# Winograd block products: running sums in PSUM and all operand sums on VectorE

## The chip, the core and the metric

The kernel runs on one core of one Trainium2 chip. The time is the device time of one launch in microseconds (us). Three timed runs of the kernel before took 3626.16, 3637.07 and 3639.25 us, median 3637.07. The engines are named as in the profile: PE is TensorE's matmuls and PEld its weight loads, DVE is VectorE, ACT is ScalarE, POOL is GpSimd, SP is SyncE, which issues the loads.

## The reference, cut to what matters

Two transformer-like blocks, one after the other, on 1024 tokens of 1024 features in float32. The ten stretches that this document is about are three matrix products with 1024 output features: the down products of the three feed-forward nets, and the output product of the second block's mixer.

```python
# block 1
x = x + einsum("bte,ed->btd", mix, w_out)                # mix: gating, convolution, delta rule
h = rms_norm(x, ffn_norm_g)
ff = silu(h @ w_gate) * (h @ w_up)                       # 1024 -> 2816 features
x = x + ff @ w_down                                      # first down: 2816 -> 1024
x = rms_norm(x, final_norm_g)
# block 2
h = concatenate([meta_tokens, x])                        # 16 tokens more
h = h + 0.5 * swiglu(rmsnorm(h, ffn1_norm), w1, w3, w2)  # second down
...
h = h + merged @ w_out                                   # merged: attention and state space, gated
h = h + 0.5 * swiglu(rmsnorm(h, ffn2_norm), w1, w3, w2)  # third down
return rmsnorm(h, final_norm)[:, 16:]
```

## The kernel before

**Precision.** Every float32 operand is split in two parts, hi + lo: ScalarE copies it to a rounded hi, VectorE subtracts hi to get lo (`hilo`, L208 to L210; `wsplit`, L245 to L254, for weights). A product is then three matmuls, hi hi, hi lo and lo hi, for each of the 128-feature tiles of the inner sum (`product`, L460 to L468; the matmul is L467).

**Block products.** Tokens are kept as two halves of 512, features on the partitions. A product with 1024 outputs is a 2 x 2 block product (output halves r, inner halves c, token halves h), and `seven` computes it in Winograd's form: seven block products in place of eight, at the price of sums of weight blocks A[r, c] and of feature blocks B[c, h]. The down products are cut into three batches of 4, 3 and 4 feature tiles per inner half; the mixer's output product is one batch of 4. Each of a batch's seven products gives four output tiles of 128 features; with four inner tiles such a tile is 4 x 3 = 12 matmuls of 512 columns. The batches are called here a1, a2, a3 (first down), b1, b2, b3 (second down), c (mixer's output product) and d1, d2, d3 (third down). In the second down the 16 extra tokens make the first half 528 long, and every tile goes in two pieces of 264 columns.

**Operand sums.** `both` (L500 to L503, the sum itself is L503) makes a sum two inner tiles at a time, so 128x1024 (or 128x1056 for 528 tokens); they are called from `prepare` (L505 on), which makes the operands of a product while the one before it runs. `pools` (above `wblock`) says on which engine ten of the sixteen sums of a batch go: VectorE in a1 and a2, GpSimd in the other eight batches. Weight blocks are loaded into the pools `raw` and `s`, feature blocks into `s`; the next batch's are loaded into the slots of the blocks that have been used up.

**Residual sums.** Each output tile's product lies in a PSUM bank and is added to the residual tiles in SBUF, `hs[half][r]` (`add`, L579 to L583; L581 is the plain sum, L583 the one with a factor). Winograd's form needs partial sums that go to more than one place: a tile x in SBUF takes product 1 by a ScalarE copy (L608), then 6 and 7 are added into it, and x is added to residuals from there. Per output tile that is nine adds on VectorE and two on the engine in `pools`. The PSUM buffers `pd` (three) and `pq` (three) take turns; `ps` (two) is used by other steps, among them the state space's matrices, which are traced beside the first feed-forward net.

**Beside it.** In the last batch of each product, finished residual tiles go to the sums of squares of the next norm (`Stat`, its add on GpSimd is L98; the norm's factors come from matmuls at L404 to L409), and in d3 through the final norm's transposes (`Final`, L108). A scheduler fixes each engine's instruction order when the kernel is built; each engine then runs its list in order.

## Time and profile before

| | |
|---|---|
| timed runs, median (lowest to highest) | 3637.07 us (3626.16 to 3639.25) |
| profiled execution, span | 3629.7 us |
| PE busy | 93% |
| DVE busy | 73% |
| POOL busy | 30% |

No time besides the span is recorded for the profiled execution; the median lies 7.4 us above that span. Shares are averages over the whole program, and the ten batches take 916 us of it together. For each batch a table below gives the busy time of the engines in that stretch, with the number of instructions in brackets, the mean granted clock of TensorE (PEclk, 1.00 is 2.4 GHz) and the load on the DMA engines. A row of grouped instructions gives line, engine, operation, output and inputs with their shapes, the count, the busy time of all of them and the mean of one in ns, and after the second bar the idle time ahead of them with what ended it. Rows of the timeline give start and length in us, and in square brackets how long the engine had waited, and for what.

### The profile page before, as it was taken

How to read it: one execution, taken by the hardware profiler on the slowest of the kernel's cores; microseconds unless marked ns; L12 is line 12 of the kernel's file. 1: busy time of each engine (PE TensorE's matmuls, PEld its weight loads, DVE VectorE, ACT ScalarE, POOL GpSimd, SP SyncE). 2: the span in 40 equal slices, each digit the busy share in tenths (PEclk: the TensorE clock that was granted, in tenths of full speed). 3: DMA queues.
4: the chain of work that ended last, by engine and by line, in shares of the span. 5: the costliest groups of instructions: out<-in, count | busy, mean ns of one | idle time of the engine just before them, and what ended most of it. 6: DMA issues, size and time to landing. Idle time of an engine off the chain costs nothing.

```text
span 3629.7 us, 49236 instructions
## 1 busy us (share of the span) xinstructions
PE 3387.2 (93%) x18860; PEld 2877.8 (79%) x18860; DVE 2632.0 (73%) x4371; ACT 1398.0 (39%) x2408; POOL 1091.8 (30%) x1199
## 2 busy tenths in 40 slices
PE   7989889999997978999999899999999889999988
PEld 6777777788886858999989888778777678888766
DVE  6886675866776998767689845644665986666997
ACT  4355344433332424333333435543554343333333
POOL 2332323200048254000045627300820740000555
PEclk9989999999998988999999999999999999999999
DMA  3312313222244312333353143136225222224321
GB/s 102 101 52 67 97 62 126 80 85 87 82 163 133 125 59 73 104 112 99 118 183 113 47 104 104 62 125 166 73 67 165 98 75 98 76 91 156 124 87 47
DMA packets 325097, 361.78 MB, mean 100 GB/s; under 512 B 43193, under 2 KB 240990, under 8 KB 324862
## 3 DMA queue, kind: packets, MB, share of 16 engines
q1 hardware_dynamic: 324862, 358.64, 31.0%
q8 instruction: 148, 2.42, 0.3%
q14 instruction: 87, 0.71, 0.1%
HBM read 282.75 MB, written 75.84 MB: 99 GB/s over the span
## 4 chain that ended last, share of the span: by engine, by line
PE 64%; DVE 19%; POOL 5%; issue 4%; ACT 2%; DMA 1%; SPq 0%; ACTq 0%; DVEq 0%; POOLq 0%
PE pd L467 35%; PE pd L277 16%; PE pq L467 4%; DVE wl L210 3%; DVE z L210 3%; DVE s L503 2%; DVE s L583 1%; DVE s L581 1%; DVE s L1377 1%; PE pq L1953 1%; PE pq L1993 1%; ACT wh L209 1%; POOL u L98 1%; DVE s L210 1%; PE pq L1952 1%
## 5 line engine op out<-in xcount | busy, mean ns | idle before, releaser
L277 PE MATMUL pd<-s,wh 128*128 128x512 f32 (+2 forms) x2720 | 859.6, 394 | 11.0 <-POOL s L210 5.4
L467 PE MATMUL pd<-z,wh 128*128 128x512 f32 (+1 forms) x2640 | 681.3, 346 | 40.7 <-DVE z L210 25.1
L209 ACT CAST wh<-raw 128x1024 fp32r<-128x1024 f32 (+1 forms) x424 | 439.5, 1039 | 680.6 <-PE pd L277 261.2
L210 DVE TENSOR_TENSOR wl<-raw,wh 128x1024 fp32r<-128x1024 f32 (+1 forms) x394 | 514.0, 1304 | 238.2 <-ACT wh L209 218.2
L467 PE MATMUL pd<-s,wh 128*128 128x512 f32 (+1 forms) x2560 | 635.2, 338 | 14.6 <-ACT wh L209 14.4
L277 PEld LDWEIGHTS pd<-s,wh 128*128 128x128 f32 x2720 | 508.8, 193 | 112.6 <-POOL s L210 6.7
L467 PEld LDWEIGHTS pd<-z,wh 128*128 128x128 f32 x2640 | 464.5, 193 | 103.5 <-DVE z L210 30.6
L277 PE MATMUL pd<-s,wl 128*128 128x512 f32 (+2 forms) x1360 | 534.4, 393 | 6.6 <-DVE wl L210 6.6
L467 PEld LDWEIGHTS pd<-s,wh 128*128 128x128 f32 x2560 | 440.4, 189 | 66.2 <-ACT wh L209 15.7
L467 PE MATMUL pd<-z,wl 128*128 128x512 f32 (+1 forms) x1320 | 455.6, 345 | 7.3 <-DVE wl L210 7.3
L467 PE MATMUL pd<-s,wl 128*128 128x512 f32 (+1 forms) x1280 | 432.9, 338 | 0.8 <-DVE wl L210 0.8
L467 PE MATMUL pq<-z,wh 128*128 128x512 f32 (+2 forms) x1360 | 357.7, 352 | 29.8 <-DVE s L583 22.8
L277 PEld LDWEIGHTS pd<-s,wl 128*128 128x128 f32 x1360 | 262.5, 193 | 55.1 <-DVE wl L210 7.4
L467 PEld LDWEIGHTS pq<-z,wh 128*128 128x128 f32 x1360 | 243.0, 196 | 61.3 <-DVE s L583 23.4
L467 PEld LDWEIGHTS pd<-z,wl 128*128 128x128 f32 x1320 | 254.3, 193 | 37.4 <-DVE wl L210 10.3
L467 PEld LDWEIGHTS pd<-s,wl 128*128 128x128 f32 x1280 | 241.6, 189 | 26.8 <-DVE wl L210 1.5
L467 PE MATMUL pq<-z,wl 128*128 128x512 f32 (+2 forms) x680 | 236.3, 347 | 0.0
L210 DVE TENSOR_TENSOR z<-s,z 128x1024 fp32r<-128x1024 f32 (+3 forms) x140 | 211.2, 1525 | 3.6 <-ACT z L209 3.6
L503 POOL TENSOR_TENSOR raw<-raw,s 128x1024 f32<-128x1024 f32 (+1 forms) x16 | 47.1, 2964 | 524.6 <-DMA s<-in_ffn_w_dram 398.6
L467 PE MATMUL pd<-s 128*128 128x512 f32 (+1 forms) x912 | 171.0, 336 | 0.0
L209 ACT CAST z<-s 128x1024 fp32r<-128x1024 f32 (+3 forms) x140 | 133.4, 989 | 74.3 <-DVE s L503 57.7
L98 POOL TENSOR_TENSOR u<-u,t 128x512 f32<-128x512 f32 (+4 forms) x95 | 124.8, 1321 | 114.6 <-ACT t L96 113.4
(470 smaller groups left out, 5373.9 us busy)
## 6 DMA issues: line engine op xcount, KB each, us to landing
raw<-in_w_in_dram SPq DMA_DIRECT2D x56, 1024.0 KB
raw<-in_ffn_w_dram SPq DMA_DIRECT2D x56, 1024.0 KB
ffd<-t SPq DMA_DIRECT2D x90, 256.0 KB
s<-ffd SPq DMA_DIRECT2D x16, 1024.0 KB
raw<-in_w_gate_dram SPq DMA_DIRECT2D x12, 1024.0 KB
raw<-in_w_up_dram SPq DMA_DIRECT2D x12, 1024.0 KB
raw<-in_w_out_dram SPq DMA_DIRECT2D x10, 1024.0 KB
s<-hd SPq DMA_DIRECT2D x10, 1024.0 KB
```

Source lines behind the costliest of these rows:

```text
L98: nc.gpsimd.tensor_tensor(acc, acc, s, op=ALU.add)
L209: self.nc.scalar.copy(hi, src)
L210: (eng or self.nc.vector).tensor_tensor(lo, src, hi.bitcast(F32), op=ALU.subtract)
L277: nc.tensor.matmul(out, a[:, k, :], b, start=c == 0, stop=c == 3 * kt - 1)
L467: self.nc.tensor.matmul(p[:, :n], a[:, k, :], b[:, k, t0 : t0 + n], start=c == 0, stop=c == 3 * kt - 1)
L503: eng.tensor_tensor(out[:, k], x[:, k], y[:, k], op=op)
L581: (eng or nc.vector).tensor_tensor(d, p, d, op=ALU.add)
L583: nc.vector.scalar_tensor_tensor(d, p, factor, d, op0=ALU.mult, op1=ALU.add)
L1377: nc.vector.scalar_tensor_tensor(a, y, f, a, op0=ALU.mult, op1=ALU.add)
L1952: nc.tensor.matmul(p[:, lo:272], Q[:, r, :], khi[:, cols], start=True, stop=False)
L1953: nc.tensor.matmul(p[:, lo:272], Q[hb : hb + 64, r, :], klo[hb : hb + 64, cols], start=False, stop=True)
L1993: nc.tensor.matmul(po[rr * 64 : rr * 64 + 64, j * 128 : (j + 1) * 128], v[b + s][:, g * 64 : (g + 1) * 64], PT[j][:, s, rr, :], start=Fals ...
```

## The change

It has three parts. First, where tokens go in one piece (a, c and d; `chained`), the products come in the order 1, 2, 6, 7, 4, 5, 3 (it was 1, 2, 4, 6, 7, 5, 3), and the results add up in PSUM: products 1, 6, 7 and 4 of an output tile go into one bank (`sums`, from pd, pd, pq, pq for the four tiles), 2 into another and 5 and 3 into one (`pairs`, from pd, pq, ps, ps). After each product its bank, with all that it holds by then, is added to one residual tile; there is no tile x, no copy into it, and there are seven adds per output tile. The operand sums are arranged anew for this order, with a further tile t1 = A10 + A11. Second, all operand sums are on VectorE, in all batches. Third, all residual sums are on VectorE too, also in the second down, which otherwise keeps the old form. The loads of the next batch stand at other products, and those of the second half's residual earlier. Most of the diff's remaining lines remove comments.

```diff
+        chained = len(pieces) == 1
+        order = (1, 2, 6, 7, 4, 5, 3) if chained else (1, 2, 4, 6, 7, 5, 3)
-        pools = [nc.vector if self.nff == 1 and z + 1 < len(batches) else nc.gpsimd for z in range(len(batches))]
...
-        def both(out, x, y, op, eng=nc.vector):
+        def both(out, x, y, op):
...
-                eng.tensor_tensor(out[:, k], x[:, k], y[:, k], op=op)
+                nc.vector.tensor_tensor(out[:, k], x[:, k], y[:, k], op=op)
+        def early(z):
+            t1[z] = self.S()[:, : batches[z] * 512].rearrange("p (k f) -> p k f", f=512)
+            both(t1[z], a[z, 1, 0], a[z, 1, 1], ALU.add)
...
-            if z == 0 and i == 4:
+            if z == 0 and i == (6 if chained else 4):
                 start(0, 1)
-            if z == 0 and i == 6:
+            if z == 0 and i == (2 if chained else 6):
                 start(1, 0)
                 start(1, 1)
...
+                wk = {1: (0, 0), 2: (0, 1), 6: (0, 0), 7: (1, 0), 4: (1, 1), 5: None, 3: (0, 1)}[i]
...
+            wv = A(*wk) if wk else t1[z]
...
+            if chained:
+                if i == 1:
+                    both(B(0, 0), B(0, 1), B(0, 0), ALU.subtract)
+                    early(z)
+                if i == 2:
+                    t2[z] = tile(kt)
+                    both(t2[z], B(1, 1), B(0, 0), ALU.subtract)
+                    both(A(1, 0), A(0, 0), A(1, 0), ALU.subtract)
+                    both(A(0, 0), t1[z], A(0, 0), ALU.subtract)
+                if i == 6:
+                    both(B(0, 1), B(1, 1), B(0, 1), ALU.subtract)
+                    both(B(1, 0), B(1, 0), t2[z], ALU.subtract)
+                if i == 7:
+                    both(A(0, 1), A(0, 1), A(0, 0), ALU.subtract)
+                    a[z, 0, 0] = t2[z] = None
+                    if nxt:
+                        wblock(nxt, 0, 0)
+                        fblock(nxt, 0, 0)
+                if i == 4:
+                    a[z, 1, 0] = b[z, 0, 1] = None
+                    if nxt:
+                        fblock(nxt, 1, 0)
+                        wblock(nxt, 0, 1)
+                if i == 5:
+                    a[z, 1, 1] = b[z, 1, 0] = None
+                    if nxt:
+                        wblock(nxt, 1, 1)
+                        fblock(nxt, 0, 1)
+                if i == 3:
+                    t1[z] = a[z, 0, 1] = b[z, 0, 0] = b[z, 1, 1] = None
+                    if nxt:
+                        wblock(nxt, 1, 0)
+                        fblock(nxt, 1, 1)
...
+                if chained:
+                    if i == 1:
+                        sums[u] = self.pd() if u < 2 else self.pq()
+                    if i in (2, 5):
+                        pairs[u] = (self.pd, self.pq, self.ps, self.ps)[u]()
+                    p = (sums if i in (1, 6, 7, 4) else pairs)[u]
+                    p = self.product(p, w, cur["x"], ta, n, batches[z], i in (1, 2, 5), i in (2, 4, 3), ta)
+                else:
+                    p = self.product(self.pd() if c % 2 else self.pq(), w, cur["x"], ta, n, batches[z])
...
+                if chained:
+                    add({1: ha, 2: ha, 4: ha}.get(i, hb)({1: 0, 2: 0, 6: 0, 7: 1, 4: 1, 5: 1, 3: 0}[i]), p)
...
                     elif i == 6:
                         add(s, p)
-                        add(hb(0), s[:, v:], pools[z])
+                        add(hb(0), s[:, v:], True)
                     elif i == 7:
                         add(s, p)
-                        add(ha(1), s, nc.vector)
-                        add(hb(1), s[:, v:], pools[z])
+                        add(ha(1), s, True)
+                        add(hb(1), s[:, v:], True)
```

The next two fences are VectorE's order at the start of d1, while product 1 runs and 2 begins: before, then after. L503 and L510 are the operand sums, L583 and L634 the adds to the residual, L210 the subtraction of a split, L816 and L885 the last of the gating.

```order
L583 SCALAR_TENSOR_TENSOR s<-pd,s 128x512
L816 TENSOR_TENSOR t<-t,u 128x512
L503 TENSOR_TENSOR s<-s 128x1024
L210 TENSOR_TENSOR wl<-s,wh 128x1024
L583 SCALAR_TENSOR_TENSOR s<-pq,s 128x512
L503 TENSOR_TENSOR s<-s 128x1024 x3
L583 SCALAR_TENSOR_TENSOR s<-pd,s 128x512
```

```order
L510 TENSOR_TENSOR s<-s,raw 128x1024
L885 TENSOR_TENSOR t<-t,u 128x512
L510 TENSOR_TENSOR s<-s,raw 128x1024
L634 SCALAR_TENSOR_TENSOR s<-pd,s 128x512
L210 TENSOR_TENSOR z<-s,z 128x1024 x2
L634 SCALAR_TENSOR_TENSOR s<-pd,s 128x512
L210 TENSOR_TENSOR wl<-s,wh 128x1024
L510 TENSOR_TENSOR s<-s 128x1024 x2
L510 TENSOR_TENSOR s<-raw,s 128x1024 x2
L510 TENSOR_TENSOR raw<-s,raw 128x1024 x2
L634 SCALAR_TENSOR_TENSOR s<-pq,s 128x512 x2
```

Eight operand sums stand here in place of four, and two of the residual adds wait behind six of them.

GpSimd's order in the third down, before and after; L98 is the add of squares, L746 and L210 belong to the gating's operands.

```order
L210 TENSOR_TENSOR s<-t,s 128x512
L503 TENSOR_TENSOR raw<-raw,s 128x1024 x2
L503 TENSOR_TENSOR s<-s,raw 128x1024 x2
L503 TENSOR_TENSOR s<-s 128x1024 x2
L503 TENSOR_TENSOR raw<-raw 128x1024 x2
L503 TENSOR_TENSOR s<-s,raw 128x1024 x2
L581 TENSOR_TENSOR s<-s 128x512 x8
```

```order
L746 TENSOR_TENSOR t<-s 128x512
L210 TENSOR_TENSOR s<-t,s 128x512
L98 TENSOR_TENSOR u<-u,t 128x512 x6
L98 TENSOR_TENSOR u<-u,t 128x256 x12
L2349 UNCONDITIONAL_BRANCH
```

Of three batches' sums nothing is left on GpSimd; between the gating and the squares of the last norm it has no work.

VectorE's order at the start of b2, where the form stays: before, then after.

```order
L210 TENSOR_TENSOR wl<-raw,wh 128x768
L583 SCALAR_TENSOR_TENSOR s<-pd,s 128x264
L210 TENSOR_TENSOR z<-s,z 128x1056
L210 TENSOR_TENSOR z<-s,z 128x528
L583 SCALAR_TENSOR_TENSOR s<-pq,s 128x248
L503 TENSOR_TENSOR s<-s 128x1056
L583 SCALAR_TENSOR_TENSOR s<-pd,s 128x264
L503 TENSOR_TENSOR s<-s 128x528
L583 SCALAR_TENSOR_TENSOR s<-pq,s 128x248
L210 TENSOR_TENSOR wl<-raw,wh 128x768
```

```order
L210 TENSOR_TENSOR wl<-raw,wh 128x768
L634 SCALAR_TENSOR_TENSOR s<-pd,s 128x264
L210 TENSOR_TENSOR z<-s,z 128x1056
L210 TENSOR_TENSOR z<-s,z 128x528
L634 SCALAR_TENSOR_TENSOR s<-pq,s 128x248
L634 SCALAR_TENSOR_TENSOR s<-pd,s 128x264
L510 TENSOR_TENSOR s<-s 128x1056
L634 SCALAR_TENSOR_TENSOR s<-pq,s 128x248
L210 TENSOR_TENSOR wl<-raw,wh 128x768
L634 SCALAR_TENSOR_TENSOR s<-pd,s 128x264
L510 TENSOR_TENSOR s<-s 128x528
L510 TENSOR_TENSOR raw<-raw,s 128x1024
```

The operand sums stand among the adds as before, and the weight sums (`raw<-raw,s`), which were GpSimd's, follow them.

## Rows read from the trace of the kernel before

**Rows 1.** The page, part 1: busy us, share of the span, instructions.

```profile
PE 3387.2 (93%) x18860; PEld 2877.8 (79%) x18860; DVE 2632.0 (73%) x4371; ACT 1398.0 (39%) x2408; POOL 1091.8 (30%) x1199
```

**Rows 2.** Windows, a1 to d3: length, busy PE, PEld, DVE, ACT, POOL, PEclk, DMA, GB/s.

```profile
1069.30:1193.70 124.40, 101.86 (x487) 84.45 (x486) 92.40 (x103) 34.95 (x53) 96.75 (x143) 0.89 0.45 144
1193.70:1251.80 58.10, 57.82 (x255) 47.56 (x254) 58.10 (x81) 25.61 (x33) 0.00 (x0) 1.00 0.46 156
1251.80:1368.00 116.20, 89.69 (x360) 72.52 (x359) 107.45 (x105) 38.46 (x50) 69.52 (x31) 0.88 0.14 46
1844.80:1937.50 92.70, 84.28 (x675) 83.15 (x675) 90.67 (x112) 29.82 (x37) 55.19 (x28) 0.98 0.45 149
1937.50:2009.70 72.20, 65.84 (x507) 65.01 (x506) 68.23 (x108) 26.05 (x36) 35.08 (x25) 0.95 0.31 104
2009.70:2101.00 91.30, 77.20 (x592) 76.48 (x592) 77.41 (x102) 37.36 (x64) 67.59 (x52) 0.91 0.14 47
2812.40:2911.00 98.60, 83.97 (x345) 67.18 (x344) 88.90 (x86) 37.33 (x47) 68.48 (x31) 0.91 0.27 96
3357.20:3442.90 85.70, 78.86 (x337) 64.30 (x336) 85.60 (x73) 26.39 (x29) 49.93 (x19) 0.96 0.39 133
3442.90:3509.30 66.40, 59.03 (x254) 46.96 (x254) 64.91 (x68) 24.90 (x33) 36.29 (x17) 1.00 0.35 119
3509.30:3620.00 110.70, 96.60 (x471) 79.18 (x469) 96.86 (x129) 38.57 (x55) 65.03 (x36) 0.94 0.05 20
```

**Rows 3.** Windows, stretches of d1 and b1 in which TensorE is never idle.

```profile
3404.90:3442.90 38.00, 38.00 (x169) 31.50 (x168) 37.90 (x39) 12.16 (x13) 18.95 (x9) 1.00 0.39 130
1890.90:1936.00 45.10, 45.10 (x374) 45.10 (x373) 43.07 (x66) 15.38 (x16) 18.91 (x19) 1.00 0.36 113
```

**Rows 4.** Groups on VectorE in a2, shapes kept apart: count, busy us, mean ns.

```profile
L581 DVE TENSOR_TENSOR s<-pq,s 128x512 f32<-128x512 f32 x15 | 10.0, 676 | 0.0
L210 DVE TENSOR_TENSOR z<-s,z 128x1024 fp32r<-128x1024 f32 x8 | 9.6, 1211 | 0.0
L210 DVE TENSOR_TENSOR wl<-raw,wh 128x768 fp32r<-128x768 f32 x6 | 5.7, 946 | 0.0
L503 DVE TENSOR_TENSOR s<-s 128x1024 f32<-128x1024 f32 x3 | 3.7, 1219 | 0.0
```

**Rows 5.** Groups on VectorE in d1 and d2, shapes kept apart.

```profile
L210 DVE TENSOR_TENSOR z<-s,z 128x1024 fp32r<-128x1024 f32 x20 | 32.6, 1638 | 0.0
L583 DVE SCALAR_TENSOR_TENSOR s<-pd,s 128x512 f32<-128x512 f32 x31 | 20.7, 676 | 0.0
L503 DVE TENSOR_TENSOR s<-s 128x1024 f32<-128x1024 f32 x9 | 20.0, 2243 | 0.0
```

**Rows 6.** Timeline, a stretch of b3: start, length, what, wait before it.

```profile
2018.77 0.42 DVE L583 SCALAR_TENSOR_TENSOR s<-pq,s 128x264 f32<-128x264 f32 x1
2019.12 0.41 DVE L583 SCALAR_TENSOR_TENSOR s<-pd,s 128x264 f32<-128x264 f32 x1
...
2022.30 3.32 POOL L503 TENSOR_TENSOR s<-s 128x1056 f32<-128x1056 f32 x1 [1.19 <-DVE s L503]
2023.28 8.00 DVE L503 TENSOR_TENSOR s<-s 128x1056 f32<-128x1056 f32 x3
2026.82 3.35 POOL L503 TENSOR_TENSOR s<-s 128x1056 f32<-128x1056 f32 x1 [1.20 <-DVE s L503]
...
2031.68 0.81 PE L467 MATMUL pq<-z,wh 128*128 128x264 f32 x2 [8.75 <-DVE s L583]
```

**Rows 7.** Waits of TensorE in b1 to b3: all us, count, longest.

```profile
PE pq L467 <- DVE s L583: 22.8, 9, 8.8
```

**Rows 8.** The chain that ended last, in order of time, end of a3.

```profile
1330.52 1.36 POOL s L581
...
1337.89 3.57 PE pq L409 x16
```

**Rows 9.** Windows, line L503 alone, whole span: DVE busy, then POOL busy.

```profile
0.00:3629.70 3629.70, 122.85 (x80) 230.88 (x80) 0.96 0.31 100
```

More of the change, by code (lines that the diff above doesn't have):

```diff
@@ L460, in norm_steps, with product @@
             yield from self.norm_apply(h, g, rB, t0, rB.shape[1], A)
-    def product(self, p, w, x, t0, n, kt=4):
+    def product(self, p, w, x, t0, n, kt=4, first=True, last=True, o=0):
         c = 0
@@ L466, in product @@
             for a, b in ((w[0], x[0]), (w[0], x[1]), (w[1], x[0])):
-                self.nc.tensor.matmul(p[:, :n], a[:, k, :], b[:, k, t0 : t0 + n], start=c == 0, stop=c == 3 * kt - 1)
+                self.nc.tensor.matmul(p[:, o : o + n], a[:, k, :], b[:, k, t0 : t0 + n], start=first and c == 0,
+                                      stop=last and c == 3 * kt - 1, skip_group_check=not (first and last))
                 c += 1
-        return p[:, :n]
+        return p[:, o : o + n]
     def seven(self, batches, weight, feature, residual, hs, pieces, factor, parts=None):
@@ L544, in prepare @@
             wv = xv = None
+            if chained:
[31 more added lines that the diff above has]
+                        fblock(nxt, 1, 1)
+                yield
+                return
             if i == 2:
@@ L557, in prepare @@
             if i == 6:
-                both(A(0, 1), A(0, 1), A(1, 1), ALU.subtract, pool)
+                both(A(0, 1), A(0, 1), A(1, 1), ALU.subtract)
                 t2[z] = a[z, 1, 1] = None
@@ L577, in prepare, with add @@
             yield
-        def add(d, p, eng=None):
-            if eng or factor == 1.0:
-                (eng or nc.vector).tensor_tensor(d, p, d, op=ALU.add)
+        def add(d, p, plain=False):
+            if plain or factor == 1.0:
+                nc.vector.tensor_tensor(d, p, d, op=ALU.add)
             else:
                 nc.vector.scalar_tensor_tensor(d, p, factor, d, op0=ALU.mult, op1=ALU.add)
-        items = [(z, i) for z in range(len(batches)) for i in (1, 2, 4, 6, 7, 5, 3)]
+        items = [(z, i) for z in range(len(batches)) for i in order]
         res, c = {}, 0
         drain(prepare(0, 1, res))
-        x = res.pop("X")
+        x = res.pop("X", None)
+        sums, pairs = {}, {}
         for e, (z, i) in enumerate(items):
@@ L591, in seven @@
             pre = prepare(*items[e + 1], res) if e + 1 < len(items) else iter(())
-            if i == 1 and z:
+            if i == 1 and z and not chained:
                 x = tile(4)
@@ L605, in seven @@
                 hb = lambda r: hs[1][r][:, u, tb + v : tb + n]
-                s = x[:, u, ta : ta + n] if i in (1, 6, 7) else None
-                if i == 1:
-                    nc.scalar.mul(s, p, factor)
-                    add(ha(0), p)
-                elif i == 2:
-                    add(ha(0), p)
-                elif i == 4:
-                    add(ha(1), p)
-                elif i == 6:
-                    add(s, p)
-                    add(hb(0), s[:, v:], pools[z])
-                elif i == 7:
-                    add(s, p)
-                    add(ha(1), s, nc.vector)
-                    add(hb(1), s[:, v:], pools[z])
-                elif i == 5:
-                    add(hb(1), p[:, v:])
-                    add(hb(0), p[:, v:])
-                else:
-                    add(hb(0), p[:, v:])
-                s = None
+                if chained:
+                    add({1: ha, 2: ha, 4: ha}.get(i, hb)({1: 0, 2: 0, 6: 0, 7: 1, 4: 1, 5: 1, 3: 0}[i]), p)
+                    if i == 4:
+                        sums[u] = None
+                    if i in (2, 3):
+                        pairs[u] = None if i == 2 or ta + n == 512 else pairs[u]
+                else:
+                    s = x[:, u, ta : ta + n] if i in (1, 6, 7) else None
+                    if i == 1:
+                        nc.scalar.mul(s, p, factor)
+                        add(ha(0), p)
+                    elif i == 2:
+                        add(ha(0), p)
+                    elif i == 4:
+                        add(ha(1), p)
+                    elif i == 6:
+                        add(s, p)
+                        add(hb(0), s[:, v:], True)
+                    elif i == 7:
+                        add(s, p)
+                        add(ha(1), s, True)
+                        add(hb(1), s[:, v:], True)
+                    elif i == 5:
+                        add(hb(1), p[:, v:])
+                        add(hb(0), p[:, v:])
+                    else:
+                        add(hb(0), p[:, v:])
+                    s = None
+                p = None
                 if u == 1 and tb + n == 512:
@@ L631, in seven @@
                         next(pre, None)
-                yield i if last else 0, u, ra, rb
+                yield ({7: 4, 4: 7}.get(i, i) if chained else i) if last else 0, u, ra, rb
             cur = None
```

22 lines of the change are left out of this document (11 added, 11 removed).

## The prediction

> **What bounds the kernel now.** I read the shares first, then a table of the ten batches of block products in question, then the stretches in which TensorE runs undisturbed, then VectorE's operations one by one, once without and once beside GpSimd. The shares [rows 1] call TensorE the bound: 93% busy, VectorE 73%, GpSimd 30%. But the shares average over the program, and the change touches ten batches only: three of the first feed-forward block (a1 to a3), three of the second (b1 to b3), one of the mixer's output product (c), three of the third block (d1 to d3). In their table [rows 2] VectorE is the crowded one: busy for 85.60 of 85.70 us in d1, 90.67 of 92.70 in b1, 107.45 of 116.20 in a3.
>
> What would TensorE need? In undisturbed stretches 168 matmuls of 512 columns take 38.0 us and 372 of 264 columns 45.1 us [rows 3], so 0.226 and 0.121 each (the x counts there include the one cut by the edge). A batch with four feature tiles has 7 products of 4 tiles of 12 matmuls, 336: a floor of 76.0 us. With three tiles it is 252: 57.0. In the second block, in two pieces of 264, the floors are 81.5 and 61.1. Against these the batches lose [rows 2]: a1 48.4, a2 1.1, a3 40.2, b1 11.2, b2 11.1, b3 9.8, c 22.6, d1 9.7, d2 9.4, d3 34.7; all but a1 and a2: 148.7 us. (a1's loss is largely the state space's matrices traced beside it; a3's, c's and d3's hold norms and transposes too.)
>
> Why is VectorE crowded? Without GpSimd at work, in a2, a hi/lo subtraction of 128x1024 takes 1211 ns and an operand sum 1219 [rows 4]. In d1 and d2, beside GpSimd's sums, the same subtraction takes 1638 and the same sum 2243, while an add that reads one operand from PSUM keeps its 676 [rows 5]. So only operations with both inputs in SBUF stretch. One place shows it [rows 6]: three sums, worth 3 x 1.2 = 3.7 us alone, take 8.00 while GpSimd runs sums of 3.32 and 3.35 us, and TensorE has stood still for 8.75 us when it resumes at 2031.68, waiting for the add behind them. Over b1 to b3 TensorE waits 22.8 us for such adds [rows 7]. GpSimd's queue costs in a second way: in a3's chain the norm's matmuls at 1337.89 follow residual sums on GpSimd [rows 8].
>
> **What is removed.** Of GpSimd: 80 operand sums, busy 230.9 us (blocked time included) [rows 9], in eight batches (a3, b1 to b3, c, d1 to d3; a1 and a2 had theirs on VectorE already), and 88 residual sums of the line below. Of VectorE, in the seven chained batches (a, c, d): the nine adds per output tile (eleven in a1 and a2, which had the residual sums too) become seven: 8 adds x 0.676 = 5.4 us less per batch [rows 4], 10.8 in a1 and a2. Of ScalarE 4 copies into x per batch, which no row shows on the path: nothing.
>
> **What is added to VectorE.** Ten sums in each of the eight batches: 10 x 1.22 = 12.2 us with four tiles. In the second block also GpSimd's two residual sums per piece: 16 x 0.42 = 6.7 us per batch.
>
> **Does it fit?** Operations overlap: the adds at 2018.77 and 2019.12 last 0.42 and start 0.35 apart [rows 6], so one counts about 0.08 less than it lasts. Three tiles, chained: a2 is nearly this case, with all sums on VectorE, no GpSimd and eleven adds, and TensorE lost 1.1 us [rows 2]; the change takes 10.8 us of adds from it, and d2 after the change has the same sums as a2 now and four adds per tile fewer. Four tiles, chained: 28 splits and 16 sums, 44 x 1.21 = 53.2, and 28 adds x 0.676 = 18.9: 72.1, less 72 x 0.08: 66.3, against TensorE's 76.0. Fits with a tenth to spare. Second block, four tiles: 44 x 1.23 (half of them of 1056) = 54.1 and 88 adds x 0.42 = 37.0: 91.1, less 132 x 0.08: 80.5, against 81.5: level. Three tiles there: splits 14 x 0.95 + 7 x (1.25 + 0.69), sums 4 x 1.90 + 4 x 1.94, adds 37.0: 79.2, less 10.6: 68.6 against 61.1, so VectorE becomes the bound of b2. (0.95 for 768 columns is a row [rows 4]; 1.25 for 1056 and 0.69 for 528 are estimates in proportion to 1.211 for 1024 and 0.676 for 512 [rows 4], and 1.90 is a weight sum of 1024 columns and one of 512.)
>
> **The terms.** The sums cluster. In a chained batch VectorE gets six sums while product 1 runs and four more in product 2: 4 x 1.13 + 4 x 0.60 + 6 x 1.13 = 13.7 us in product 1 (each less its 0.08), against TensorE's 10.9. I allow 4 us of such stalls per batch, with a little slow clock behind them, 3 with three tiles.
> - a3: the stalls between products 1 and 2 and before the norm shrink, and the granted clock (0.88 of 2.4 GHz now [rows 2]) rises with them: -15.
> - b1: VectorE's 80.5 plus 4 to 5: 85; -7.5. b2: 68.6 plus 1.5: 70; -2. b3 (granted clock 0.91): 86; -5.
> - c: -8. Here and in a3 and b3 the squares' adds on GpSimd no longer stand behind sums.
> - d1: 76.0 + 5: -4.5. d2: 57.0 + 3: -6. d3: -8; its final transposes share one bank of three with the held sums, so not more.
> - a1 and a2: 0. In a1 the state space's products want the banks ps that the new pairs hold; bounds -10 (fewer adds) to +12 (a quarter of its loss again).
>
> Loads: their number is the same. The next batch's last weights now feed a sum that VectorE takes in order; behind it wait the splits of product 3 and all adds. Some 7 us of VectorE work lie between the freeing of the slot and that sum, so I take 0; if a load is late by half a product, 5 us at each of four batch starts, 20 us. The earlier residual loads of the second half are issued at nearly the same place: nothing.
>
> Sum: 15 + 7.5 + 2 + 5 + 8 + 4.5 + 6 + 8 = 56 us. Own bounds of the parts: no part gains more than its loss (148.7), and each could give back its added VectorE work. The sum is made against the profiled execution's span, 3629.7 us; the median of the three timed runs is 7.4 above it, and I carry that over: 3637 - 56 = 3581.
>
> **Rivals.**
> Banks (slower). The chained form holds all eight PSUM banks, four running sums and four pairs. A product may go on in a tile's bank only when the add of the product before has read it, three tiles later: 3 x 2.71 = 8.1 us (6.1 with three tiles). Before, six buffers rotated: five tiles, 13.6 us. If VectorE lags further than that at the handovers 6 to 7, 7 to 4 and 5 to 3, TensorE stands there: 21 handovers; from 3.7 us each the change loses over 0.5%. It would give about 3637 - 56 + 21 x 3.7 = 3659. For it: VectorE is level or worse in product 1 and 2. Against it: those two use separate banks, and during 6, 7, 4 and 5 VectorE has 7 to 9 us of work per 10.9.
> The Trainium skill (PSUM — Partial Sum Buffer, Summary: rules for kernel authors) says that a bank is to be read while matmuls target a different one, which here means a wait at each of these handovers. No row of before has a bank handed over in this way.
>
> VectorE bound (no change). d1 holds 28 splits, 6 sums and 36 adds on VectorE, 41.5 + 24.3 less 5.6 = 60.2 us by the unstretched times, and it was busy 85.60 [rows 2]: some 25 us are stretching and leftovers of the gating. In b1 it is 34.4 + 7.5 + 30.1 less 8.5 = 63.5 against 90.67: 27. If only a quarter of that is GpSimd's doing, d1 needs 66.3 + 19 = 85, as now; b1 80.5 + 20 = 100, 8 more than now, b2 and b3 some 5 more each; the others keep about 8 of their gain: 3637 + 18 - 8 = 3647 at the worst, near 3637 if half is. Against it: a2's rows, where nothing was stretched.
>
> All of it. If nearly every wait in the eight batches came from GpSimd's stretching: -90 to -110, about 3540. For it: in b and d almost every wait of TensorE is for VectorE. Against it: norms, transposes and clusters of sums stay.
> The Trainium skill (SBUF — State Buffer, Who interferes with whom) calls the shared port an exclusive lock: a VectorE operation with two SBUF inputs and a GpSimd one that reads SBUF exclude each other for a whole instruction. By that rule every stretched operation of rows 5 goes back to its time of rows 4, which is this rival's premise; rows 6 agree (8.00 for 3.7), and rows 5 for the operand from PSUM.
>
> The change does not do what it says: GpSimd keeps the adds of squares and in a1 the matrices, so some stretching stays there; that lies within a1's bounds.
>
> **How the numbers follow.** Forecast 0.62; all of it 0.15; VectorE bound 0.14; banks (or late loads) 0.09. A measurement of this kernel tells 0.5%, 18 us, from no change. Faster: forecast and all of it, and a little of the third: 0.80. Same 0.12, slower 0.08. Predicted 3581. The likeliest case alone spans 3553 to 3609 (each term halved or raised by half); the range that leaves out two in ten, with half of all-of-it and most of the third, is 3540 to 3634.
>
> **What would show it.** GpSimd's busy time falls by the 231 us of rows 9 and its residual sums on top, and no two-input operation of 128x1024 on VectorE in d1 or d2 averages above 1.25 us. VectorE's share stays about where it is (more work, less stretching). d1 and d2 last about 81 and 60 us, b1 to b3 about 85, 70 and 86, with VectorE full in b2. Waits of TensorE for an add of the first or second block's kind lie at product starts, not at the handovers of banks. Wrong if TensorE's longest waits in chained batches are at products 7, 4 or 3 for a PSUM add, if b1 to b3 together exceed 256 us, or if the two-input operations stay stretched without GpSimd.

## The result, and the profile after

The changed kernel takes 3551.76 us, the median of five runs (3532.02 to 3554.1), against 3630.56 for the kernel before in the same comparison: ratio 0.977, 95% interval 0.9742 to 0.9799, so 79 us less. Faster by 56 us to 3581 was forecast, with 3540 to 3634 as the range. The direction and the range held; the time lies 1 us below the likeliest case's own range (3553 to 3609) and nearer to the rival "all of it" (3540) than to 3581.

The profiled execution of the changed kernel is the fastest of its five: span 3530.3 us, 99 below that of before. Ten of these 99 us are not the change's. In one stretch ahead of a1, which both kernels run alike, the granted clock was 0.77 of 2.4 GHz on average in the execution before (so some of it at the lower level, 1.2) and 1.00 in the one after. The change is not behind it: of the eleven other kernels below three have the short form of this stretch in their profile and eight the long one, and kernels made from the one before (vec_early short, vec_only long) and from the changed one (a1_old_form short, idle_adds long) are on both sides. Length, busy times and clock of that stretch, first in the kernel before, then in the one after:

```profile
192.73:243.66 50.93, 45.30 (x402) 37.78 (x400) 39.57 (x72) 21.95 (x42) 16.42 (x11) 0.77 0.08 24
```

```profile
194.15:235.15 41.00, 35.21 (x402) 29.05 (x401) 38.60 (x70) 21.58 (x42) 16.86 (x11) 1.00 0.10 29
```

So whole spans are poor evidence at this size, and the batches are compared one by one below, from the first matmul of one to the first of the next. Together the ten shorten by 95.2 us in these two executions; the medians' 79 us is what five runs of each support. The page of the changed kernel, part 1 (against [rows 1]):

```profile
PE 3350.3 (95%) x18860; PEld 2852.3 (81%) x18860; DVE 2540.5 (72%) x4427; ACT 1384.5 (39%) x2380; POOL 742.3 (21%) x1031
```

GpSimd is busy 349.5 us less. VectorE does more operations (4427, it was 4371) in less time. The ten batches a1 to d3 in the changed kernel, with the columns of [rows 2]:

```profile
1061.55:1195.34 133.79, 104.13 (x486) 85.89 (x484) 82.08 (x91) 33.58 (x49) 87.78 (x143) 0.87 0.46 143
1195.34:1252.46 57.12, 57.12 (x254) 47.33 (x252) 54.75 (x68) 22.87 (x29) 0.00 (x0) 1.00 0.39 136
1252.46:1340.22 87.76, 83.66 (x361) 68.00 (x360) 83.47 (x101) 36.40 (x46) 24.82 (x13) 0.96 0.19 61
1817.19:1908.43 91.24, 85.02 (x676) 84.60 (x674) 87.61 (x144) 30.06 (x37) 0.00 (x0) 0.96 0.45 151
1908.43:1972.88 64.45, 62.37 (x507) 61.90 (x505) 64.28 (x124) 26.16 (x36) 0.00 (x0) 1.00 0.35 117
1972.88:2053.20 80.32, 74.20 (x593) 73.51 (x592) 79.59 (x128) 36.84 (x63) 31.09 (x25) 0.98 0.16 54
2767.05:2846.76 79.71, 77.88 (x344) 64.28 (x343) 74.36 (x86) 35.05 (x42) 24.10 (x13) 0.98 0.33 118
3294.36:3372.31 77.95, 76.77 (x338) 62.92 (x336) 74.99 (x85) 24.47 (x26) 0.00 (x0) 1.00 0.43 146
3372.31:3429.43 57.12, 57.12 (x254) 47.33 (x252) 53.93 (x68) 22.90 (x29) 0.00 (x0) 1.00 0.40 138
3429.43:3522.14 92.71, 90.91 (x480) 76.62 (x479) 79.03 (x130) 38.05 (x54) 23.44 (x18) 0.98 0.06 23
```

d2 and a2 now run at TensorE's floor (57.12 for 57.0), d1 2 us above its own. VectorE is full in b2 and b3 (64.28 of 64.45 and 79.59 of 80.32 us) and nearly so in b1. a1 is the only batch that became longer. VectorE's groups in d1 and d2 of the changed kernel (against [rows 5]):

```profile
L210 DVE TENSOR_TENSOR z<-s,z 128x1024 fp32r<-128x1024 f32 x21 | 25.1, 1221 | 0.0
L634 DVE SCALAR_TENSOR_TENSOR s<-pd,s 128x512 f32<-128x512 f32 x22 | 15.1, 686 | 0.1
L510 DVE TENSOR_TENSOR s<-s 128x1024 f32<-128x1024 f32 x12 | 14.3, 1220 | 0.0
```

The subtraction went from 1638 to 1221 ns and the operand sum from 2243 to 1220, the values that stood in a2 before [rows 4]. All operand sums, of the whole program (against [rows 9], where 80 on VectorE took 122.85 and 80 on GpSimd 230.88):

```profile
0.00:3530.30 3530.30, 179.31 (x160) 0.98 0.32 102
```

Twice as many sums on VectorE cost it 56 us more in all.

### The profile page after: what moved, and what is told of

Read it like the earlier page. It is cut to its first block, busy times and chain, and to the rows that moved or that the text cites. A ratio compares the mean times of both kernels' runs of the same rounds, so it can differ in the third digit from the quotient of the medians.

```text
span 3530.3 us, 49007 instructions
## 1 busy us (share of the span) xinstructions
PE 3350.3 (95%) x18860; PEld 2852.3 (81%) x18860; DVE 2540.5 (72%) x4427; ACT 1384.5 (39%) x2380; POOL 742.3 (21%) x1031
## 4 chain that ended last, share of the span: by engine, by line
PE 68%; DVE 18%; POOL 3%; issue 2%; DMA 2%; ACT 2%; SPq 0%; ACTq 0%; DVEq 0%; POOLq 0%
PE pd L468 36%; PE pd L277 16%; PE pq L468 5%; DVE wl L210 3%; DVE z L210 2%; DVE s L510 2%; PE ps L468 2%; DVE s L1446 1%; DVE s L634 1%; PE pq L2022 1%; PE pq L2062 1%; PE pq L2021 1%; ACT wh L209 1%; DVE s L210 1%; DVE s L632 1%
## 5 line engine op out<-in xcount | busy, mean ns | idle before, releaser
L277 PE MATMUL pd<-s,wh 128*128 128x512 f32 (+2 forms) x2720 | 857.7, 394 | 11.1 <-POOL s L210 6.4
L210 DVE TENSOR_TENSOR wl<-raw,wh 128x1024 fp32r<-128x1024 f32 (+1 forms) x380 | 474.7, 1249 | 215.2 <-ACT wh L209 196.0
L468 PE MATMUL pd<-z,wh 128*128 128x512 f32 (+1 forms) x2476 | 617.7, 338 | 4.3 <-DVE z L210 3.5
L468 PEld LDWEIGHTS pd<-z,wh 128*128 128x128 f32 x2476 | 427.9, 190 | 53.7 <-DVE z L210 5.4
L468 PE MATMUL pd<-z,wl 128*128 128x512 f32 (+1 forms) x1238 | 419.0, 338 | 0.0
L98 POOL TENSOR_TENSOR u<-u,t 128x512 f32<-128x512 f32 (+4 forms) x95 | 136.2, 1442 | 1185.4 <-ACT t L96 1184.5
L468 PE MATMUL pq<-z,wh 128*128 128x264 f32 (+1 forms) x1196 | 303.7, 343 | 18.4 <-DVE s L634 14.1
L468 PEld LDWEIGHTS pd<-z,wl 128*128 128x128 f32 x1238 | 234.9, 190 | 23.7
L468 PEld LDWEIGHTS pq<-z,wh 128*128 128x128 f32 x1196 | 208.5, 193 | 43.2 <-DVE s L634 14.5
L468 PE MATMUL pq<-z,wl 128*128 128x264 f32 (+2 forms) x598 | 203.4, 340 | 0.0
L210 DVE TENSOR_TENSOR z<-s,z 128x1024 fp32r<-128x1024 f32 (+3 forms) x140 | 166.6, 1214 | 12.9 <-ACT z L209 12.8
L468 PEld LDWEIGHTS pd<-s 128*128 128x128 f32 x912 | 143.5, 188 | 17.7
```

What stands on the lines that cost most here:

```text
L98: nc.gpsimd.tensor_tensor(acc, acc, s, op=ALU.add)
L210: (eng or self.nc.vector).tensor_tensor(lo, src, hi.bitcast(F32), op=ALU.subtract)
L277: nc.tensor.matmul(out, a[:, k, :], b, start=c == 0, stop=c == 3 * kt - 1)
L468: self.nc.tensor.matmul(p[:, o : o + n], a[:, k, :], b[:, k, t0 : t0 + n], start=first and c == 0, stop=last and c == 3 * kt - 1, skip_gro ...
```

## The experiments

Eleven further kernels ran. The table gives each batch's length in us in its one profiled execution, up to the same instruction in all (d3 of before ends here at 3621.29 and is 112.0, where [rows 2] cut it at 3620.0), and the sum of the ten. As in [rows 2], b3 ends with 91 of its 672 matmuls still to come, and c with some 8.

| kernel | a1 | a2 | a3 | b1 | b2 | b3 | c | d1 | d2 | d3 | sum |
|---|---|---|---|---|---|---|---|---|---|---|---|
| before | 124.3 | 57.7 | 116.6 | 92.7 | 72.2 | 91.4 | 98.5 | 85.7 | 66.3 | 112.0 | 917.4 |
| changed | 133.8 | 57.1 | 87.8 | 91.2 | 64.5 | 80.3 | 79.7 | 78.0 | 57.1 | 92.7 | 822.2 |
| vec_only | 124.5 | 57.8 | 111.7 | 89.7 | 64.5 | 80.3 | 86.0 | 77.2 | 62.5 | 110.8 | 865.0 |
| chain_only | 137.1 | 57.1 | 92.4 | 92.8 | 71.1 | 93.2 | 88.8 | 93.1 | 57.9 | 105.7 | 889.2 |
| second_net_old | 136.2 | 57.1 | 86.2 | 92.8 | 70.8 | 93.1 | 80.4 | 78.0 | 57.1 | 93.0 | 844.7 |
| idle_sums | 136.7 | 57.1 | 87.8 | 92.3 | 64.4 | 81.7 | 92.5 | 92.8 | 63.2 | 108.1 | 876.6 |
| idle_memsets | 135.9 | 57.1 | 86.2 | 91.2 | 64.4 | 81.8 | 87.9 | 78.0 | 57.1 | 91.4 | 831.0 |
| idle_adds | 134.9 | 57.1 | 96.0 | 91.2 | 64.4 | 81.7 | 88.4 | 79.2 | 60.2 | 98.2 | 851.3 |
| residuals_only | 124.5 | 57.7 | 115.9 | 92.7 | 68.5 | 88.8 | 93.9 | 85.8 | 64.5 | 109.3 | 901.6 |
| vec_early | 130.0 | 57.1 | 110.8 | 91.1 | 64.3 | 81.7 | 85.8 | 77.0 | 62.6 | 106.5 | 866.9 |
| a1_old_form | 125.3 | 57.1 | 89.2 | 89.7 | 64.4 | 80.3 | 79.9 | 78.0 | 57.1 | 92.7 | 813.7 |
| a1_old_early | 129.5 | 57.1 | 88.7 | 89.9 | 64.3 | 83.2 | 80.0 | 78.0 | 57.1 | 93.0 | 820.8 |
| a1_old_squares | 124.6 | 57.1 | 81.8 | 90.1 | 64.4 | 82.8 | 78.0 | 77.9 | 57.1 | 89.3 | 803.1 |

Where kernels run a batch alike, its lengths agree within 3.3 us in a1, 3 in a3, 2.6 in b1, 1.8 in b3, 1.4 in b2 and 0.7 elsewhere; a difference no larger than this says nothing.

**Each part alone: vec_only and chain_only.** The first is the kernel before with one line changed; the second is the changed kernel with the operand sums that were moved, and the second net's residual sums, back on GpSimd.

```diff
-        pools = [nc.vector if self.nff == 1 and z + 1 < len(batches) else nc.gpsimd for z in range(len(batches))]
+        pools = [nc.vector for z in range(len(batches))]
```

> The kernel before with all its operand and residual sums on VectorE and nothing else: the old product order, the tile x and its copies stay. Theory 'sharing' (what was lost is VectorE's two-input operations stretching beside GpSimd): two thirds or more of the gain of 79 us is there without the chained form, 3560 to 3580 us, with a hi/lo subtraction of 128x1024 at 1.21 to 1.25 us in d1 and d2. Rival 'chained form' (fewer adds and running sums in PSUM bring the gain; more sums on VectorE alone crowd it): 3610 us or more. The second feed-forward net is then the same as in the changed kernel: b1 to b3 within 3 us of its 235 us under both.

```diff
-                    both(A(1, 0), A(0, 0), A(1, 0), ALU.subtract)
-                    both(A(0, 0), t1[z], A(0, 0), ALU.subtract)
+                    both(A(1, 0), A(0, 0), A(1, 0), ALU.subtract, pool)
+                    both(A(0, 0), t1[z], A(0, 0), ALU.subtract, pool)
...
-                        add(hb(1), s[:, v:], True)
+                        add(hb(1), s[:, v:], pools[z])
```

> The changed kernel with ten operand sums per batch (A10, A00, B01, B10, A01) on GpSimd again in a3, c and d1 to d3, and the second feed-forward net wholly as before: the chained form without the move to VectorE. 'Sharing': only the adds and copies saved show, 3600 to 3625 us, and the subtractions of d1 and d2 average above 1.5 us again. 'Chained form': 3575 us or less in spite of the stretching.

vec_only took 3584.23 us, ratio 0.9862 (0.9825 to 0.99), some 50 us; chain_only 3609.67, ratio 0.9927 (0.9902 to 0.9952), some 27. So neither theory has it all: by these ratios some 60% of the gain come with the move to VectorE and 30% with the chained form (vec_only missed the expected 3580 by 4 us). In the sums of the table they give 52 and 28 of 95 us, and the last 15 come only with both. They work in different batches. d1's gain is wholly the move's (77.2; the chained form alone makes it longer, 93.1), and so are those of b2 and b3. d2 and a3 gain mostly by the chained form. In d3 either part alone gives 1 to 6 us and both together 19. The batch windows of d1, d2 and d3 in vec_only (columns as above):

```profile
3328.04:3405.21 77.17, 76.46 (x338) 63.00 (x337) 76.05 (x91) 26.47 (x30) 0.00 (x0) 1.00 0.45 148
3405.21:3467.70 62.49, 58.79 (x254) 47.02 (x252) 62.23 (x84) 25.02 (x33) 0.00 (x0) 1.00 0.37 127
3467.70:3578.55 110.85, 97.08 (x481) 80.19 (x479) 97.97 (x154) 40.40 (x58) 20.83 (x18) 0.94 0.05 20
```

In d2 VectorE is busy for 62.23 of 62.49 us although nothing stretches it: there the adds are too many for the time, and the chained form, which takes 16 operations out (84 to 68), lets TensorE reach its floor.

**second_net_old.** The changed kernel, with the second net alone as before (the `pool` arguments and `pools[z]` of the diff above, in the old form's branch only).

> The changed kernel with the second feed-forward net alone as before (operand and residual sums on GpSimd as they were). In the trace of the changed kernel b1 to b3 gave 1.5, 7.7 and 11 us, 20 in all. 'Sharing': these 20 us come back, 3565 to 3577 us. Rival (the second net's gain is the granted clock of that one execution, since VectorE is the bound there either way): within 8 us of the changed kernel.

It took 3566.54 us, ratio 0.9805 (0.9761 to 0.985): 15 us above the changed kernel by the medians, 20.7 in the windows of b1 to b3. That is what "sharing" forecast; no other batch moved by more than its scatter.

**Is it the sharing? idle_sums and idle_memsets.** Both leave the changed kernel's work as it is and add work on GpSimd that nobody uses, paced by reading the sums just made.

```diff
+        def idle(v):
+            if junk is not None:
+                for k in range(4):
+                    nc.gpsimd.tensor_tensor(junk, v[:, k % v.shape[1], 0:512], junk, op=ALU.add)
...
                     both(A(1, 0), A(0, 0), A(1, 0), ALU.subtract)
+                    idle(A(1, 0))
```

> The changed kernel with sums on GpSimd that nobody uses: behind each of the five moved operand sums of c, d1, d2 and d3 GpSimd adds four 128x512 slices of the sum into a scratch tile of its own, as many elements as the two sums that it had there before. Nothing on the path waits for them except the squares' adds behind them on GpSimd. 'Sharing': c and d1 to d3 give back most of their 55 us, 25 to 45 us in all, the subtractions beside them above 1.5 us. Rival 'queue' (the gain is that GpSimd's own results come sooner): only c and d3 grow, together under 15 us, d1 and d2 within 1.5 us. Rival 'chained form': under 8 us in all.

In idle_memsets the body of `idle` is this instead:

```diff
+                nc.gpsimd.tensor_tensor(junk[:, 0:16], v[:, 0, 0:16], junk[:, 0:16], op=ALU.add)
+                for k in range(12):
+                    nc.gpsimd.memset(junk, 0.0)
```

> As the kernel with idle GpSimd sums, but at each of those places GpSimd reads only a 128x16 slice of the sum and then sets its scratch tile twelve times (128x512 each), so it is busy and reads almost nothing. With the idle sums c, d1, d2 and d3 lasted 92.5, 92.8, 63.2 and 108.1 us, without 79.7, 78.0, 57.1 and 92.7. If what stretches VectorE is GpSimd's reading of SBUF: at most 5 us of those 49 come back, d1 and d2 within 1 us of 78.0 and 57.1. If any GpSimd instruction does it: 25 us or more.

With idle sums the kernel took 3598.18 us (ratio 0.9913, 0.9881 to 0.9945), 46 above the changed one; c and the three d batches lost 49 us of the 55 that the change had given them (25 to 45 were expected). With memsets it took 3560.81 (one run), and d1 and d2 stayed at 78.0 and 57.1. The windows of d1, first with the sums, then with the memsets:

```profile
3331.32:3424.12 92.80, 81.06 (x338) 65.25 (x337) 92.59 (x84) 24.55 (x26) 49.56 (x24) 0.94 0.36 123
```

```profile
3324.39:3402.35 77.96, 76.80 (x337) 62.90 (x336) 74.99 (x85) 24.48 (x26) 49.26 (x78) 1.00 0.43 147
```

GpSimd is busy for as long (49.56 and 49.26 us) and VectorE has the same work, yet it is busy for 92.59 us in the one and 74.99 in the other. The subtractions of d1 and d2, sums first:

```profile
L210 DVE TENSOR_TENSOR z<-s,z 128x1024 fp32r<-128x1024 f32 x20 | 35.8, 1808 | 0.0
```

```profile
L210 DVE TENSOR_TENSOR z<-s,z 128x1024 fp32r<-128x1024 f32 x21 | 25.2, 1224 | 0.0
```

So it is not that GpSimd is busy, but what it does: sums that read SBUF stretch VectorE's, memsets don't. The Trainium skill (SBUF — State Buffer, Who interferes with whom) says just this: two SBUF inputs on VectorE contend with a GpSimd instruction that reads SBUF, not with one that only writes it. These rows agree. Of the 49 us, 6.9 stay with the memsets, where at most 5 were expected, and they are all in c: 87.9, 8.2 above the changed kernel, while VectorE is not slower (72.14 us busy, it was 74.36). There the squares' adds stand behind memsets in GpSimd's queue: five squares' adds (L98) start at 2853.04 us, when the last twelve memsets are done, and TensorE's matmuls of the norm (L396) wait 7.8 us for L98, a wait that the changed kernel's c does not have. So this rest is GpSimd's queue, not VectorE.

**Fewer adds, or the form? idle_adds.** The changed kernel with four idle adds per output tile on VectorE.

```diff
+                    if i in (6, 7, 5):
+                        idle(z, hb(0 if i == 6 else 1), 2 if i == 7 else 1)
```

> The changed kernel with four idle adds per output tile on VectorE in a3, c and d1 to d3 (128x512 each, of a residual tile into a scratch tile: one after products 6 and 5, two after 7), which is what the chained form took from VectorE against the old form with all sums on it. Theory 'VectorE is full in the last batches': a3, c and d3 grow by 6 to 11 us each (16 adds x 0.676 = 10.8), d1 and d2 by under 2, in all 20 to 33. Rival 'form' (the order of the products and the sums in PSUM save the time, not the adds): under 8 us in all.

It took 3580.0 us (one run). a3 grew by 8.2, c by 8.7, d1 by 1.2, d2 by 3.1 and d3 by 5.5 us, 26.7 in all, as the theory had it (d2 a little more, d3 a little less). In the last batches most of an add's time on VectorE is time of the batch: 5.5 to 8.7 of 10.8 us. It leaves a rest, though: with as many adds as vec_only, a3 is still 15.7 us shorter than there and d3 12.6, c 2.4 longer.

**residuals_only.** The kernel before, with the two residual sums alone on VectorE (`nc.vector` for `pools[z]` in both adds).

> The kernel before with only its residual sums taken from GpSimd to VectorE; the operand sums stay on GpSimd. Theory 'queue' (a3's 24 us of gain in the chained form with GpSimd's operand sums came because the norm no longer follows residual sums on GpSimd): a3 falls from 116.6 to 105 or less, c and d3 by 5 or more each. Rival 'fewer adds and operands' : a3, c, d3 within 4 us of before, in sum no gain.

It took 3614.77 us (one run). a3 hardly moved (115.9), so "queue" falls for a3: taking residual sums from GpSimd's queue does not bring its norm forward. c gained 4.6, b2 3.7, b3 2.6, d3 2.7, 16 us in all batches, so the rival's "no gain" does not hold either.

**vec_early.** vec_only with two sums earlier, to test whether a3's and d3's rest is a matter of when the operand sums come.

```diff
-            if i == 4:
-                both(B(1, 0), B(1, 0), t2[z], ALU.subtract)
-                yield
...
+            if i == 1:
+                both(B(0, 0), B(0, 1), B(0, 0), ALU.subtract)
             if i == 2:
                 t2[z] = tile(kt)
-                both(B(0, 0), B(0, 1), B(0, 0), ALU.subtract)
                 both(t2[z], B(1, 1), B(0, 0), ALU.subtract)
+                both(B(1, 0), B(1, 0), t2[z], ALU.subtract)
```

> All sums on VectorE in the old form, with two of them earlier: B00 = B01 - B00 made in product 1 (was 2), B10 - t2 at the end of product 2's preparation (was the first thing of product 4's, ahead of its split). With all sums on VectorE alone a3 was 111.7, c 86.0 and d3 110.8 us; with the chained form and as many adds on VectorE 96.0, 88.4 and 98.2. Theory 'spread' (the rest of the chained form's gain in a3 and d3 is that its operand sums come earlier and none stands ahead of a split): a3 falls by 6 us or more, and a3, c, d3 together by 10 or more. Rival (it is the sums in PSUM and the order of products themselves): a3 within 3 us of 111.7, all three together within 6.

It took 3584.06 us, ratio 0.9872 (0.9842 to 0.9902), the same as vec_only; a3 took 110.8, and a3, c and d3 gained 5.4 together, 4.3 of it in d3. "Spread" falls. What the trace of vec_only shows at the end of its a3 is another thing: the steps that make the norm's factors (L413 to L222, short ones) stand in VectorE's queue between the old form's adds (L581). VectorE's timeline there (start, length):

```profile
1350.26 0.15 DVE L413 TENSOR_SCALAR ms<-pq 128x4 f32<-128x4 f32 x1
1350.33 0.15 DVE L414 TENSOR_SCALAR ms<-pq 128x4 f32<-128x4 f32 x1
1350.40 0.68 DVE L581 TENSOR_TENSOR s<-pd,s 128x512 f32<-128x512 f32 x1
1351.00 0.15 DVE L415 SCALAR_TENSOR_TENSOR ms<-ms 128x4 f32<-128x4 f32 x1
1351.07 0.68 DVE L581 TENSOR_TENSOR s<-pd,s 128x512 f32<-128x512 f32 x1
1351.67 0.16 DVE L216 TENSOR_SCALAR r<-ms 128x8 int32<-128x8 int32 x1
...
1352.50 1.23 DVE L220 TENSOR_TENSOR rs_a<-r 128x8 f32<-128x8 f32 x1
...
1355.75 1.23 DVE L220 TENSOR_TENSOR rs_a<-r 128x8 f32<-128x8 f32 x1
...
1359.39 1.22 DVE L220 TENSOR_TENSOR rs_a<-r 128x8 f32<-128x8 f32 x1
1360.65 0.17 DVE L221 SCALAR_TENSOR_TENSOR rs_a<-rs_a,ms 128x8 f32<-128x8 f32 x1
1360.85 0.17 DVE L222 SCALAR_TENSOR_TENSOR r<-rs_a,r 128x8 f32<-128x8 f32 x1
```

TensorE stands from 1351.25 to 1361.07 for the last of these, 9.8 us. L220, a step with both inputs in SBUF, is stretched as well: it takes 0.16 us in a1_old_squares, where GpSimd does nothing beside it, and 1.22 or 1.23 here. Each time it ends 0.02 or 0.03 us behind a squares' add on GpSimd:

```profile
1351.94 1.76 POOL L98 TENSOR_TENSOR u<-u,t 128x512 f32<-128x512 f32 x1 [2.15 <-ACT t L96]
1355.19 1.77 POOL L98 TENSOR_TENSOR u<-u,t 128x512 f32<-128x512 f32 x1 [1.49 <-ACT t L96]
1358.45 2.14 POOL L98 TENSOR_TENSOR u<-u,t 128x512 f32<-128x512 f32 x1 [1.49 <-ACT t L96]
```

In idle_adds TensorE's wait for the factors is 4.8 us, in the changed kernel 1.8 (TensorE's waits in its a3; total, count, longest):

```profile
PE pq L426 <- DVE r L222: 1.8, 1, 1.8
```

So five of the 15.7 us are this. The windows tell of most of the rest; a3 of vec_only and of idle_adds, then d3 of idle_adds (that of vec_only stands above):

```profile
1258.59:1370.29 111.70, 91.09 (x362) 73.18 (x360) 102.13 (x124) 38.64 (x50) 28.57 (x13) 0.85 0.15 48
1262.11:1358.13 96.02, 82.97 (x361) 67.31 (x359) 91.95 (x115) 35.74 (x43) 25.92 (x11) 0.96 0.20 67
3470.27:3568.44 98.17, 90.33 (x480) 75.25 (x479) 94.92 (x146) 37.46 (x52) 28.00 (x18) 1.00 0.04 16
```

For the same matmuls TensorE is busy 8.1 us less in a3 and 6.8 less in d3, at the higher clock; its waits for splits in a3 fall by another 2.9 us, and in d3 its waits with the final norm's transposes for residual adds by 4.4 (4.7 in vec_only, 0.3 in idle_adds). What in the chained form keeps these waits short and the clock high was not tried apart and stays open.

**a1: a1_old_form and a1_old_early.** The chained form is chosen batch by batch, and not in a1; in the second kernel the old form has vec_early's two sums as well.

```diff
-        chained = len(pieces) == 1
+        chain = [len(pieces) == 1 and (self.nff > 1 or z > 0) for z in range(len(batches))]
```

> The changed kernel with the old form in a1 alone, beside which the state space's matrices run; all else as changed. In all traces with the chained form a1 lasted 133.8 to 137.1 us, with the old form 124.3 and 124.5. Theory 'banks': the pairs in ps and the sums in pq hold the banks that those matrices want, so a1 goes back to 125 and the kernel gains 9 to 12 us, ratio 0.974 against before. Rival (a1 and the stretch ahead of it only trade time): within 3 us of the changed kernel.

> The changed kernel with the old form in a1, and in the old form wherever it stands (a1, b1 to b3) the two earlier sums. The same without the earlier sums took 3529.96 us, ratio 0.971. Theory 'spread': b1 to b3 lose another 4 to 8 us of their 234, ratio 0.969 to 0.970. Rival (VectorE is full there, 87 to 88 of 90 us in b1, so that moving work within a batch gives nothing): b1 to b3 within 2 us, ratio 0.971.

a1_old_form took 3529.96 us, ratio 0.971 (0.968 to 0.974), a1 125.3: the chained form is what costs a1 its 9 us. The gain by the medians, 22 us, is more than the ten batches give (8.5); the rest goes with a granted clock of 0.973 to 0.977 over its five runs, where four of the changed kernel's five had 0.967 or 0.968, and no batch explains it. The fastest runs of the two are 9.3 us apart, which is near what the batches give. That it is the banks was not shown. TensorE's waits in a1 of the changed kernel are for the matrices' own steps, 29.7 us with one more of 3.7 (in a1 before they came to 22.5, in a1_old_form to 24.0):

```profile
PE pq L1889 <- ACT u L1893: 10.0, 1, 10.0
PE ps L1872 <- POOL u L1852: 9.6, 5, 4.0
PE pq L1889 <- DVE t L1882: 6.4, 1, 6.4
```

The 10.0 us one is for a ScalarE copy that itself waited for the store of the tile it writes into (in a1_old_form the same copy waits 7.25 us for it):

```profile
1128.66 0.37 ACT L1893 COPY u<-pq 128x256 f32<-128x256 f32 x1 [9.26 <-DMA qmat<-u]
```

The 6.4 us one is the new cluster of operand sums: VectorE runs six of them in a row ahead of L1882, the matrices' add that TensorE's L1889 needs. In a1_old_form this wait is 1.6 us, so 4.8 of a1's 8.5 us go with the cluster.

```profile
1076.92 2.84 DVE L510 TENSOR_TENSOR s<-raw,s 128x1024 f32<-128x1024 f32 x2
1079.68 2.82 DVE L510 TENSOR_TENSOR s<-s 128x1024 f32<-128x1024 f32 x2
1082.43 2.82 DVE L510 TENSOR_TENSOR raw<-s,raw 128x1024 f32<-128x1024 f32 x2
1085.17 0.28 DVE L1882 TENSOR_TENSOR t<-t,ps 128x128 f32<-128x128 f32 x1
```

a1_old_early took 3544.11 us, ratio 0.9757 (0.9733 to 0.9781): b1 and b2 unchanged, a1 4.2 longer, b3 1.4 to 2.9 (its scatter is 1.8). The whole kernel is 14 us above a1_old_form, and the batches show 7 of them. Moving these sums within a batch in which VectorE is full gave nothing.

**a1_old_squares.** a1_old_form with the squares' add (L98) on `nc.vector`.

> The changed kernel with the old form in a1, and all adds of squares (128x512 and smaller pieces) on VectorE, so that GpSimd does nothing beside the last batches. Theory 'sharing' holds for the squares too: a hi/lo subtraction in a3 averaged 1491 ns beside them; unstretched, VectorE gets 12 x 0.28 us back and pays 7 to 14 adds of 0.68 for it per batch, so nothing or a loss: within 6 us of 3529.96, a3 and d3 each within 4 us. Rival 'any work on GpSimd beside VectorE costs more than it saves': 8 us less or better.

It took 3508.38 us, ratio 0.9666 (0.964 to 0.9693), the fastest of all. The rival's number holds, though not its "any work": the memsets cost VectorE nothing. a3 lost another 4.4 to 7.4 us (its lengths elsewhere being 86.2 to 89.2), d3 3.4 and c 1.9. In a3 a subtraction takes 1219 ns here, where it took this in the changed kernel beside the squares:

```profile
L210 DVE TENSOR_TENSOR z<-s,z 128x1024 fp32r<-128x1024 f32 x12 | 17.6, 1491 | 0.0
```

The theory had counted these subtractions; the squares had stretched other steps too, as L220 above. About half of the gain lies in another stretch ahead of a1, 61.65 us at a clock of 0.86 in a1_old_form and 49.66 at 1.00 here: TensorE is busy 52.41 and 46.21 us in it, and its wait for a VectorE step (L1261) falls from 7.1 to 1.7 us. In the profiles of all twelve other kernels this stretch takes 59 to 63 us, so it is hardly scatter; whether the squares there have a part in it was not tried.

## Why the prediction was right, and where its sizes were off

**The mechanism held.** VectorE's two-input operations were stretched by GpSimd's sums and went back to their own time; d1's VectorE fell from 85.60 [rows 2] to 74.99 us with ten more sums in it. In c and the d batches the idle sums bring the loss back without touching the data and the memsets leave VectorE alone, so this is shown, not argued. The rival "VectorE bound" fails on the same number: of d1's 25 us which I would not assign between stretching and leftovers, 10.6 + 12.2 - 5.4 = 17.4 were stretching (what it is less busy, and the sums added less the adds removed).

**Three-tile batches.** a2 as the model for d2 was right: 57.1 (forecast 60).

**Second net.** Its sum was near (236.0 us; forecast 85 + 70 + 86 = 241), its distribution not. b1 kept VectorE full for 87.6 us where 80.5 was worked out: 144 operations run in its window, not the 132 counted, since the gating's last and b2's first are among them. In b2 and b3 124 and 128 run. For b3 the forecast also misread its row: the window in [rows 2] ends before 91 of b3's 672 matmuls, so that a floor of 81.5 us did not belong to its 91.3. For the 581 in it the floor is about 70 and the loss 21, not 9.8; measured are 80.3 us, a gain of 11.1 that the bound "no part gains more than its loss" excluded.

**The last batches, a3, c and d3, were mis-sized.** The terms were -15, -8 and -8, together 31 us; they measured -28.8, -18.8 and -19.3, together 67, and this is most of what the forecast lacked. By the experiments the move to VectorE alone gives 18.6 of the 67 (vec_only), the 16 adds per batch that the chained form does without there 22.4 (idle_adds), and 25.9 are the rest of the chained form (15.7 in a3, 12.6 in d3, c 2.4 longer). What the forecast had too small is the price of an add in these batches: it counted stalls at product starts and the norm's place in GpSimd's queue. But VectorE has the norm's work beside the last products as well and is the busiest engine there (107.45 of 116.20 us in a3 before [rows 2]), and the norm's steps wait among its adds. Taking the residual sums out of GpSimd's queue gained 0.7 us in a3 (residuals_only). And the clock, which a3's term names without a size and c's and d3's leave out, is 19 us of the 67, spread over these shares: for the same matmuls TensorE is busy 90.08 us in a3 before (to the same instruction) and 83.66 after, at 0.88 and 0.96; in c 83.97 and 77.88, at 0.91 and 0.98; in d3 97.72 and 90.91, at 0.94 and 0.98.

**The total** lies in the range partly by luck: these 36 us too few were in part offset by a1's loss, and by the medians, which show 16 us less than the ten batches of the profiled executions do.

**a1** cost 9.5 us, for which 0 stood with bounds of -10 to +12. The place was right, but not the cause as far as it is known: of the waits that grew, 4.8 us are for a matrices' step behind clustered sums. Whether the rest comes of banks no row decides.

**The rival "banks" did not come about.** In a3 the only wait of a product for an add of a residual was 0.5 us, in c there was none, in d1 to d3 one of 0.2. The 8 us of slack were enough. The rule of the Trainium skill (PSUM — Partial Sum Buffer, Summary: rules for kernel authors) that would have put a wait at each handover did no harm here: as the missing waits show, the add of three tiles before was done by then.

**"All of it"** came nearer to the median than the forecast did. Its premise, that every stretched operation goes back, was borne out in d1 and d2, but not in a3, where the squares' adds stay on GpSimd and a subtraction still averaged 1491 ns; its limit, that clusters stay, showed in a1.

## What to carry to other kernels

Where VectorE is full, look at the mean time of its operations by shape, beside GpSimd's work and without it: a helper engine that reads the same memory can take more from VectorE than it does for it, and here even the adds of squares were cheaper on the full engine. Price an operation removed from the busiest engine of a stretch by its length (here half to four fifths of it was time), and add the clock that fewer stalls give back. Where small steps on the path (a norm's factors, the side work of another stage) share a queue with bulk sums, look at what stands ahead of them before bunching the sums, and at what another engine runs beside them. And before a floor is set against a window, count that the window holds all of the work.
